# First projection of a hybrid encoder layer: input and weight loads in turn, dummy matmuls ahead, parameters turned behind the loop

## The chip, the core and the metric

The kernel runs on one core of one Trainium2 chip. The metric is device time in microseconds (us) of that core, from the runtime's own clock; a profiled execution has a span (first to last instruction) a little shorter than its time. Engines: TensorE (PE, with its weight loads as PEld), VectorE (DVE), ScalarE (ACT), GpSimd (POOL) and SyncE (SP), which issues most loads.

## The reference

One layer of a streaming encoder runs on two request groups that share the weights: a prompt of 256 positions and 32 sampled positions, 288 columns in all. Everything is float32.

```
xn   = rmsnorm(x, norm_mix_pre)
proj = xn @ w_in      # [u_pool 1024 | z 2048 | xBC 2560 | dt 32]
pool = trailing-mean mixer on u_pool (windows 2, 4, 8, 16), then w_pool
ssd  = Mamba-2 mixer: causal conv + SiLU on xBC = [xs 2048 | B 256 | C 256],
       dt = softplus(.), exact chunked scan, gate silu(z), grouped rmsnorm
x    = x + rmsnorm(concat[pool, ssd] @ w_out, norm_mix_post)
h    = rmsnorm(x, norm_ffn_pre)
x    = x + rmsnorm((silu(gate) * value) @ w_down, norm_ffn_post)
       # [gate | value] = causal conv of width 3 over h @ w_up (2 * 5632 columns)
```

Outputs are the two x and the new histories and states of the convolutions, the pooling and the scan.

## The kernel before

**Tiling.** Features lie on the 128 partitions, the 288 positions in the free dimension. A matrix product is made in three float32r matmuls per 128 x 128 weight block (`mm3`, L162 to L165: high part times high part, high times low, low times high), each with 288 columns. `split_w` (L134) makes the high part of a loaded weight tile on ACT (L146, `whi`) and the low part on DVE (L147, `wlo`); `split_from` (L113) does the same for activations (L120 on ACT, L121 on DVE). The buffers `raw`, `hi` and `lo` of the pool `wpool` come four each; a raw buffer holds 8 KB a partition, 1 MB in all.

**The first projection** gives the columns B (256), C (256) and dt (32) of `w_in`. `project` (L167) runs over five steps of k (2, 2, 4, 4 and 4 blocks of 128 features). In each step it fetches three weight tiles (`fetch_w`, L131, on SP), and before it splits them calls `first_in` for the step behind, which runs `input_tiles` (L292): load of the prompt's columns into `xt` (L294) and of the samples' into `xs_` (L295), both on SP; per 128 features three transposes on TensorE into one PSUM tile, two of 128 rows (L299, L300) and one of the samples' 32 rows (L301); the split with the gain `g_mix_pre`; a copy of the unscaled tile to `xT` (L304), stored to DRAM per step from ACT (L306). The normalization itself is applied later: the sums of squares of each position (`ssum`, L348 and L349 on ACT), root and reciprocal, and three matmuls against the identity (L355) spread them into `rstd`, by which the results are multiplied as they leave PSUM.

The dt columns go through `split_narrow`, which lays high and low part side by side so that two matmuls a k do for three (L185, L186). `parameters` (L309) turns the small parameters, which POOL loads at the start, with ten transposes (L281, L325); it is called ahead of the last step.

**Five PSUM buffers** (`acc_ps`) hold the five results of this projection. They come free as `conv_in` (L377) multiplies them by `rstd`, and only then the next projection, x's columns (`xs_ps`), can begin to accumulate. After that follow, all through `project`: x, z and u columns, the pool mixer, `w_out`, `w_up` and `w_down`.

**Order.** A planner orders the instructions of each engine by priority, readiness and its own estimate of their durations. `tc.keep_in_program_order(ins)` pins an instruction behind the one traced just before it on the same engine. Engines serve their queues in order. At the start POOL clears constants (`ident`, `ones`, `rec`, `scan_one`, `ebuf`), DVE makes `sel`, `pick` and `sel64`, and `warm` lets ACT load its table (L225).

Of the kernel before, what the change touches and what calls it, by code (L numbers as in the profile page):

```python
# [16 lines left out]
P = 128  # L17
TC = {"schedule_with_timeline_sim": True}
D_MODEL = 2048
NP_ = 256  # L20
# [17 lines left out]
EVAC = 100  # L38
SUMS_AFTER = 2
# [6 lines left out]
def body(  # L46
# [81 lines left out]
    def fetch_w(view, kb, nk, c0, nc_):  # L128
        raw = wpool.tile([P, nk, nc_], F32, tag="raw", name="raw")
        with tc.high_priority(offset=ahead[0]):  # L130
            sp.dma_start(out=raw, in_=view[:, kb : kb + nk, c0 : c0 + nc_])  # L131
        return raw

    def split_w(raw, kb, nk, nc_, after=()):  # L134
# [3 lines left out]
        for k in range(0, nk, step):  # L138
# [3 lines left out]
            with ExitStack() as order:  # L142
# [3 lines left out]
                act.activation(hi, raw[:, k : k + n, :], AF.Copy)  # L146
                dve.tensor_tensor(lo, raw[:, k : k + n, :], hi.bitcast(F32), op=ALU.subtract)  # L147
# [3 lines left out]
    def split_narrow(raw, kb, nk, nc_, after):  # L151

        both = xin.tile([P, nk, 2, nc_], F32R, tag="both", bufs=2, name="both")
        with ExitStack() as order:
            order.enter_context(tc.high_priority(offset=ahead[0]))
            for ins in after:
                order.enter_context(tc.issue_after(ins.ins))
            act.activation(both[:, :, 0, :], raw, AF.Copy)
            dve.tensor_tensor(both[:, :, 1, :], raw, both[:, :, 0, :].bitcast(F32), op=ALU.subtract)
        return [(kb + k, both[:, k, :, :].rearrange("p r c -> p (r c)")) for k in range(nk)]  # L160
# [6 lines left out]
    def project(view, groups, acts, ksplit, before=None, done=None, spare=(), hold=(), behind=None):  # L167
# [7 lines left out]
        for i, (kb, n) in enumerate(ksplit):  # L175
# [5 lines left out]
            for raw, (c0, w) in zip(raws, groups):  # L181
                if w < P:
                    for k, both in split_narrow(raw, kb, n, w, after or ()):
                        o = accs[m0][: 2 * w, :]
                        pe.matmul(o, both, acts[k][:, 0, :], start=k == k_first, stop=False)  # L185
                        pe.matmul(o, both, acts[k][:, 1, :], start=False, stop=k == k_last)  # L186
                    continue
# [33 lines left out]
    )  # L221
    eps_t = const.tile([P, 1], F32, name="eps_t")
# [10 lines left out]
    sel = const.tile([HEADS, 2], F32, name="sel")  # L233
    pick = const.tile([HEADS, NX], F32, name="pick")
    id32 = ident[:HEADS, :HEADS]
    dve.tensor_reduce(sel, id32.rearrange("h (t r) -> h r t", r=2), axis=AX.X, op=ALU.add)
    dve.tensor_reduce(pick, id32.rearrange("h (t r) -> h t r", r=2), axis=AX.X, op=ALU.add)
    sel64 = const.tile([HEADS, 2, 64], F32, name="sel64")
    dve.tensor_copy(sel64, sel.unsqueeze(2).broadcast_to([HEADS, 2, 64]))

# [6 lines left out]

    start = ExitStack()
    xin = start.enter_context(tc.tile_pool(name="xin", bufs=1))
# [9 lines left out]
    xs_ = xin.tile([NS, D_MODEL], F32, name="xs_")  # L259
# [24 lines left out]

    g_mix_pre = columns(g0_in, KD, "g0")
# [6 lines left out]
    def input_tiles(kb, n):  # L292
# [3 lines left out]
        for t in range(kb, kb + n):  # L296
            p_ = aux([P, NT], "pt")
            c = slice(t * P, (t + 1) * P)
            pe.transpose(p_[:, 0:P], xt[:, 0, c], ident)  # L299
            pe.transpose(p_[:, P:NP_], xt[:, 1, c], ident)  # L300
            pe.transpose(p_[:, NP_:NT], xs_[:, c], ident[:NS, :NS])  # L301
            a = atile("xn")
            last = split_from(a, p_, g_mix_pre[:, t : t + 1])
            dve.tensor_copy(xT[:, t, :], p_)  # L304
            xn.append(a)
# [844 lines left out]
```

## Time and profile before

| | |
|---|---|
| time, median of 3 runs | 1357.07 us (1357.01 to 1357.39) |
| profiled execution: time | 1357.63 us |
| profiled execution: span | 1355.8 us |
| TensorE busy | 1337.4 us, 99%, 10201 matmuls |
| DVE, ACT, POOL busy | 884.0, 667.0, 237.6 us (65%, 49%, 18%) |
| DMA | 252.13 MB, mean 186 GB/s |
| longest groups | L147 on DVE, 493.8 us (416 times, 1189 ns); L146 on ACT, 427.0 us (416 times, 1028 ns) |

A row of the timeline reads: start, duration, engine, line of the kernel, operation, output from inputs, shape, count. Matmuls are pipelined, so a duration is longer than the distance to the next start; the distance is what a matmul costs. A row of the windows gives, for each engine, busy us and in brackets the number of instructions, then the granted TensorE clock, the share of the DMA engines and GB/s. The chain is the work that ended last, followed back through what released each step.

### The profile page before, as it was taken

The numbers are of one execution on the slowest core, as the hardware profiler recorded it, in microseconds if no ns is written. First come the engines' busy times: TensorE is split into PE (matmuls) and PEld (weight loads), VectorE is DVE, ScalarE is ACT, GpSimd is POOL, SyncE is SP. The second block draws the span as 40 slices with busy tenths as digits, with TensorE's granted clock in tenths as the row PEclk, the third lists the DMA queues.
The fourth block names the chain that finished last, engine by engine and source line by source line (L and its number), as shares of the span: only waits on it lengthen the run. The fifth ranks groups of instructions, "written<-read, shape, count | busy, mean of one in ns | idle before, by whom it ended". The sixth has DMA issues, their size and how long they took to land.

```text
span 1355.8 us, 25731 instructions
## 1 busy us (share of the span) xinstructions
PE 1337.4 (99%) x10201; PEld 1327.3 (98%) x10201; DVE 884.0 (65%) x1515; ACT 667.0 (49%) x997; POOL 237.6 (18%) x394
## 2 busy tenths in 40 slices
PE   8999999999999999999999999999999999999996
PEld 7999999999999999999999999999999999999995
DVE  6898988779644469977666643435666667654443
ACT  6557757446534455644444433334444444454441
POOL 3132112222224310311121100001112112101110
PEclk9999999999999999999999999999999999999998
DMA  8879885565756536866545555555545545576652
GB/s 268 249 190 277 257 245 172 156 220 153 241 180 209 170 111 202 244 180 193 171 158 173 160 155 159 169 179 163 179 156 165 177 156 167 168 226 201 189 163 88
DMA packets 300136, 252.13 MB, mean 186 GB/s; under 512 B 75729, under 2 KB 293051, under 8 KB 299887
## 3 DMA queue, kind: packets, MB, share of 16 engines
q1 hardware_dynamic: 296810, 243.20, 59.2%
q0 software_dynamic: 2320, 4.65, 1.2%
q10 hardware_dynamic: 884, 2.63, 0.5%
q8 instruction: 80, 1.31, 0.4%
q14 instruction: 42, 0.34, 0.1%
HBM read 236.13 MB, written 14.31 MB: 185 GB/s over the span
## 4 chain that ended last, share of the span: by engine, by line
PE 98%; DVE 0%; DMA 0%; SPq 0%; issue 0%; DVEq 0%; ACT 0%
PE acc L163 31%; PE acc L165 31%; PE acc L164 31%; PE pst L852 1%; PE py L562 1%; DMA xt<-in_x_prompt 0%; DVE xr L1108 0%; PE acc_x L164 0%; PE acc_x L165 0%; PE acc_x L163 0%; PE py L564 0%; PE pt L301 0%; PE acc L186 0%; PE pt L299 0%; PE acc L185 0%; PE py L568 0%
## 5 line engine op out<-in xcount | busy, mean ns | idle before, releaser
L147 DVE TENSOR_TENSOR wlo<-raw,whi 128x1024 fp32r<-128x1024 f32 (+1 forms) x416 | 493.8, 1189 | 350.7 <-ACT whi L146 340.2
L146 ACT ACTIVATE whi<-raw 128x1024 fp32r<-128x1024 f32 (+1 forms) x416 | 427.0, 1028 | 505.6 <-PE acc L164 429.5
L163 PE MATMUL acc<-hn,whi 128*128 128x288 f32 x1376 | 404.6, 295 | 0.0
L164 PE MATMUL acc<-hn,whi 128*128 128x288 f32 x1376 | 403.5, 294 | 0.0
L165 PE MATMUL acc<-hn,wlo 128*128 128x288 f32 x1376 | 403.2, 294 | 0.0
L164 PEld LDWEIGHTS acc<-hn,whi 128*128 128x128 f32 x1376 | 259.8, 189 | 0.1
L165 PEld LDWEIGHTS acc<-hn,wlo 128*128 128x128 f32 x1376 | 259.6, 189 | 0.0
L163 PEld LDWEIGHTS acc<-hn,whi 128*128 128x128 f32 x1376 | 257.3, 187 | 0.1
L163 PE MATMUL acc<-xn,whi 128*128 128x288 f32 x704 | 209.5, 299 | 0.0
L163 PE MATMUL acc<-fa,whi 128*128 128x288 f32 x704 | 208.6, 296 | 0.0
L164 PE MATMUL acc<-fa,whi 128*128 128x288 f32 x704 | 208.4, 296 | 0.0
L164 PE MATMUL acc<-xn,whi 128*128 128x288 f32 x704 | 208.2, 297 | 0.0
L165 PE MATMUL acc<-fa,wlo 128*128 128x288 f32 x704 | 208.0, 295 | 0.0
L165 PE MATMUL acc<-xn,wlo 128*128 128x288 f32 x704 | 207.5, 297 | 0.0
L164 PEld LDWEIGHTS acc<-xn,whi 128*128 128x128 f32 x704 | 133.8, 190 | 0.3
L165 PEld LDWEIGHTS acc<-xn,wlo 128*128 128x128 f32 x704 | 133.2, 190 | 0.3
L163 PEld LDWEIGHTS acc<-xn,whi 128*128 128x128 f32 x704 | 132.6, 189 | 0.5
L164 PEld LDWEIGHTS acc<-fa,whi 128*128 128x128 f32 x704 | 132.7, 188 | 0.0
L163 PEld LDWEIGHTS acc<-fa,whi 128*128 128x128 f32 x704 | 132.2, 188 | 0.0
L165 PEld LDWEIGHTS acc<-fa,wlo 128*128 128x128 f32 x704 | 132.0, 188 | 0.0
L944 POOL COPY fc_stage<-ebuf 128x4 f32<-128x4 f32 x88 | 27.9, 317 | 505.7 <-DVE ebuf L943 505.7
L950 DVE SCALAR_TENSOR_TENSOR fc<-ebuf,pf,fc 128x290 f32<-128x290 f32 x176 | 90.3, 517 | 2.8 <-ACT fc L948 0.2
(310 smaller groups left out, 1621.6 us busy)
## 6 DMA issues: line engine op xcount, KB each, us to landing
raw<-in_w_up SPq DMA_DIRECT2D x80, 1024.0 KB, 5.2
raw<-in_w_in SPq DMA_DIRECT2D x40, 1024.0 KB, 6.1
raw<-in_w_down SPq DMA_DIRECT2D x32, 1024.0 KB, 5.4
raw<-in_w_out SPq DMA_DIRECT2D x24, 1024.0 KB, 5.9
raw<-in_w_down SPq DMA_DIRECT2D x16, 768.0 KB, 4.6
raw<-in_w_up SPq DMA_DIRECT2D x14, 512.0 KB, 4.2
gb<-g_d SPq DMA_DIRECT2D x8, 832.0 KB, 5.0
raw<-in_w_in SPq DMA_DIRECT2D x6, 512.0 KB, 6.5
```

The lines of the kernel that those rows point to most:

```text
L146: act.activation(hi, raw[:, k : k + n, :], AF.Copy)
L147: dve.tensor_tensor(lo, raw[:, k : k + n, :], hi.bitcast(F32), op=ALU.subtract)
L163: pe.matmul(out, wh, a[:, 0, :], start=start, stop=False)
L164: pe.matmul(out, wh, a[:, 1, :], start=False, stop=False)
L165: pe.matmul(out, wl, a[:, 0, :], start=False, stop=stop)
L562: ins = pe.matmul(y[c, 0:256], xw[:, 0, f_], m[:, h, 0:256], start=True, stop=False)
L852: ins = pe.matmul(st[:, o, :], x_, btok[:, gi, b, :], start=b != 1, stop=b != 0)
L944: pool.tensor_copy(fc_stage[:, :, :, i], e[:, 256:324].rearrange("p (s c) -> p s c", c=34)[:, :, 0:2])
L950: dve.scalar_tensor_tensor(c, e[:, r_ : r_ + 290], pf[:, r_, i : i + 1], c, op0=ALU.mult, op1=ALU.add)
```

## The change

- The first projection is written out as a loop of its own, over ten steps of k (`FIRST`: 1, 1, 1, 1, then six of 2). B and C are loaded as one tile of 512 columns. All loads are issued at the start on SP, pinned in turn: x, weights, x, weights, and so on; the rest of the samples behind the second, and all dt columns in one load behind the sixth weight load.
- The four raw buffers hold all of B and C. The dt split is made once, in the eighth step, and its matmuls follow the gathered k, then those of each step.
- The samples lie at partitions 96 to 127 of `xs_`, and zeros above them (the first two tiles' columns cleared by DVE, the others by POOL); their transpose becomes a matmul against the last 32 columns of the identity. Their first two tiles are loaded from ACT's queue.
- Twelve dummy matmuls on `busy`, a copy of `ones` made by DVE, are put on TensorE: seven ahead of the gain's transpose, five behind the first tile's.
- Tiles are turned one step ahead. In the first k the products of the high part come first, then tile 1 is turned, then the products of the low part. The first four steps are pinned on TensorE (in part), ACT and DVE.
- `xT` is stored in three pieces instead of five. `parameters` is called behind the loop, `sel`, `pick` and `sel64` are made behind it, and the three matmuls of `rstd` use all 128 rows.

```diff
+FIRST = ((0, 1), (1, 1), (2, 1), (3, 1), (4, 2), (6, 2), (8, 2), (10, 2), (12, 2), (14, 2))
+STORES = {3: 0, 9: 4, 15: 10}
+BUSY = (7, 5)
...
+    busy = xin.tile([P, NT], F32R, name="busy")
+    for o, n in BLK:
+        tc.keep_in_program_order(dve.tensor_copy(busy[:, o : o + n], ones[:, 0:n]))
+
+    xs_ = xin.tile([P, D_MODEL], F32, name="xs_")
+    tc.keep_in_program_order(dve.memset(xs_[: P - NS, : 2 * P], 0.0))
...
-    tc.keep_in_program_order(act.activation(warm, eps_t, AF.Copy))
...
+    pool.memset(xs_[: P - NS, 2 * P :], 0.0)
...
+    tc.keep_in_program_order(act.dma_start(out=xs_[P - NS :, : 2 * P], in_=x_sample[0][:, : 2 * P]))
+    tc.keep_in_program_order(act.activation(warm, eps_t, AF.Copy))
+    busy_ps = aux([P, NT], "busy_ps")
+
+    def keep_busy(n):
+
+        for _ in range(n):
+            tc.keep_in_program_order(pe.matmul(busy_ps, busy[:, 0:P], busy, start=True, stop=True))
...
+    keep_busy(BUSY[0])
     g_mix_pre = columns(g0_in, KD, "g0")
...
+    def input_load(kb, n):
         c = slice(kb * P, (kb + n) * P)
-        sp.dma_start(out=xt[:, :, c], in_=xpv[:, :, c])
-        sp.dma_start(out=xs_[:, c], in_=x_sample[0][:, c])
...
+        tc.keep_in_program_order(sp.dma_start(out=xt[:, :, c], in_=xpv[:, :, c]))
+
+    def input_tile(t):
+        p_ = aux([P, NT], "pt")
+        c = slice(t * P, (t + 1) * P)
+        pin = tc.keep_in_program_order if t < 4 else lambda ins: ins
+        pin(pe.transpose(p_[:, 0:P], xt[:, 0, c], ident))
+        pin(pe.transpose(p_[:, P:NP_], xt[:, 1, c], ident))
+        pin(pe.matmul(p_[:, NP_:NT], xs_[:, c], ident[:, P - NS :], start=True, stop=True))
+        a = atile("xn")
+        xn.append(a)
+
+        def split():
+            pin(act.activation(a[:, 0, :], p_, AF.Copy, scale=g_mix_pre[:, t : t + 1]))
+            pin(dve.scalar_tensor_tensor(
+                a[:, 1, :], p_, g_mix_pre[:, t : t + 1], a[:, 0, :].bitcast(F32), op0=ALU.mult, op1=ALU.subtract
+            ))
+
+        def keep():
+            pin(dve.tensor_copy(xT[:, t, :], p_))
+            if t in STORES:
+                c = slice(STORES[t], t + 1)
+                act.dma_start(out=xT_d[:, c, :], in_=xT[:, c, :])
+
+        return split, keep
...
+    first = [acc_ps.tile([P, NT], F32, tag="acc", name="acc") for _ in range(5)]
+    raws = [wpool.tile([P, 4, NB], F32, tag="raw", name="raw") for _ in range(4)]
+    raw_dt = xin.tile([P, KD, HEADS], F32, name="raw_dt")
+    for i, (kb, n) in enumerate(FIRST):
+        input_load(kb, n)
+        k = slice(kb, kb + n)
+        tc.keep_in_program_order(
+            sp.dma_start(out=raws[kb // 4][:, kb % 4 : kb % 4 + n, :], in_=win[:, k, O_B : O_B + NB])
+        )
+        if i == 1:
+            c = slice(2 * P, D_MODEL)
+            tc.keep_in_program_order(sp.dma_start(out=xs_[P - NS :, c], in_=x_sample[0][:, c]))
+        if i == 5:
+            tc.keep_in_program_order(sp.dma_start(out=raw_dt, in_=win[:, :, O_B + NB : O_B + NB + HEADS]))
+
+    def first_tiles(i):
+        return [input_tile(t) for t in range(FIRST[i][0], sum(FIRST[i]))] if i < len(FIRST) else []
+
+    prm = []
+    dt_parts = []
+    steps = first_tiles(0)
+    keep_busy(BUSY[1])
+    for i, (kb, n) in enumerate(FIRST):
+        pin = i < 4
+        ahead_steps = first_tiles(i + 1) if i else []
+        for split, _ in steps:
+            split()
+        parts = split_w(raws[kb // 4][:, kb % 4 : kb % 4 + n, :], kb, n, NB, pin=pin)
+        for _, keep in steps:
+            keep()
+        narrow = split_narrow(raw_dt, 0, KD, HEADS, False) if i + 3 == len(FIRST) else ()
+        dt_parts.extend(narrow)
+        if not i:
+            (_, hi, lo), = parts.pop()
+            for w, r in ((hi, 0), (hi, 1), (lo, 0)):
+                if w is lo:
+                    ahead_steps = first_tiles(1)
+                for m in range(4):
+                    tc.keep_in_program_order(pe.matmul(
+                        first[m], w[:, m * P : (m + 1) * P], xn[0][:, r, :], start=w is hi and not r, stop=False
+                    ))
+        for part in parts:
+            for m in range(4):
+                c = slice(m * P, (m + 1) * P)
+                for k, hi, lo in part:
+                    mm3(first[m], hi[:, c], lo[:, c], xn[k], k == 0, k == KD - 1)
+        while dt_parts and dt_parts[0][0] < kb + n:
+            k, both = dt_parts.pop(0)
+            o = first[4][: 2 * HEADS, :]
+            pe.matmul(o, both, xn[k][:, 0, :], start=k == 0, stop=False)
+            pe.matmul(o, both, xn[k][:, 1, :], start=False, stop=k == KD - 1)
+        steps = ahead_steps
+    prm.extend(parameters())
...
+    tc.keep_in_program_order(dve.tensor_reduce(sel, id32.rearrange("h (t r) -> h r t", r=2), axis=AX.X, op=ALU.add))
+    tc.keep_in_program_order(dve.tensor_reduce(pick, id32.rearrange("h (t r) -> h t r", r=2), axis=AX.X, op=ALU.add))
...
-            p_[:, o : o + n], rs[:n, b : b + 1].broadcast_to([n, P]), ident[:n, :n], start=True, stop=True
+        pe.matmul(p_[:, o : o + n], rs[:, b : b + 1].broadcast_to([P, P]), ident[:, P - n :], start=True, stop=True)
```

More of the change, by code (lines that the diff above doesn't have):

```diff
@@ L181, in project @@
             for raw, (c0, w) in zip(raws, groups):
[L182 to L187, printed above, removed]
                 parts = split_w(raw, kb, n, w, ((after or ()) if m0 else ()) + (hold if i else ()))
@@ L290, in body @@
     xT_d = dram.tile([P, KD, NT], F32, name="xT_d")
-    def input_tiles(kb, n):
+    def input_load(kb, n):
         c = slice(kb * P, (kb + n) * P)
-        sp.dma_start(out=xt[:, :, c], in_=xpv[:, :, c])
-        sp.dma_start(out=xs_[:, c], in_=x_sample[0][:, c])
[L296 to L305, printed above, removed]
-        act.dma_start(out=xT_d[:, kb : kb + n, :], in_=xT[:, kb : kb + n, :])
-        return last
+        tc.keep_in_program_order(sp.dma_start(out=xt[:, :, c], in_=xpv[:, :, c]))
[19 more added lines that the diff above has]
+        return split, keep
     def parameters():
```

62 lines of the change are left out of this document (27 added, 35 removed).

## The prediction

> **What bounds the kernel now.** First the page: how busy TensorE is over the span, and the chain that ended last.
>
> ```profile
> PE 1337.4 (99%) x10201; PEld 1327.3 (98%) x10201; DVE 884.0 (65%) x1515; ACT 667.0 (49%) x997; POOL 237.6 (18%) x394
> ...
> PE 98%; DVE 0%; DMA 0%; SPq 0%; issue 0%; DVEq 0%; ACT 0%
> ```
>
> TensorE is the chain. What is gained at the start moves everything behind it, as long as the stream stays fed. Then the windows of 10 us each, whose first bracket counts matmuls:
>
> ```profile
> 0.00:10.00 10.00, 4.73 (x20) 3.81 (x21) 5.77 (x12) 4.47 (x9) 8.54 (x45) 1.00 0.73 215
> 10.00:20.00 10.00, 10.00 (x61) 9.28 (x60) 6.26 (x14) 3.79 (x8) 3.38 (x7) 1.00 1.07 329
> 20.00:30.00 10.00, 10.00 (x70) 8.99 (x69) 6.45 (x13) 8.35 (x13) 0.00 (x0) 1.00 0.91 259
> 50.00:60.00 10.00, 10.00 (x77) 10.00 (x77) 8.57 (x18) 6.60 (x10) 2.85 (x5) 1.00 1.10 329
> ```
>
> The settled rate is 77 in 10 us; the first 30 us fall short of it. Busy time hides this, counts show it. Why, the chain in order of time shows (start, length):
>
> ```profile
> 6.99 0.45 PE pt L299
> ...
> 9.38 0.54 PE acc L165
> ...
> 13.23 0.24 PE acc L163
> 13.47 0.24 PE acc L164
> 13.71 0.29 PE acc L165 x2
> 14.00 0.13 PE acc L163
> ```
>
> Until 13.7 us a matmul takes 0.24 us, then 0.13: half clock. (The column of granted clock reads 1.00 there; I go by the spacing.) And from the timeline of TensorE, one input tile, then the nearest row to its new form, six matmuls of 128, 128 and 32 columns over 128 rows:
>
> ```profile
> 21.62 0.27 PE L299 MATMUL pt<-ident,xt 128*128 128x128 f32 x1
> 21.73 0.27 PE L300 MATMUL pt<-ident,xt 128*128 128x128 f32 x1
> 21.93 0.24 PE L301 MATMUL pt<-ident,xs__137 32*128 32x32 f32 x1
> 22.11 0.40 PE L165 MATMUL acc<-xn,wlo 128*128 128x288 f32 x1
> 22.35 0.29 PE L163 MATMUL acc<-xn,whi 128*128 128x288 f32 x1
> ...
> 494.13 0.39 PE L852 MATMUL pst<-btok,xw 128*128 128x128 f32 x2
> 494.36 0.81 PE L601 MATMUL rm<-ident,rm 128*128 128x128 f32 x6
> 495.00 0.47 PE L852 MATMUL pst<-btok,xw 128*128 128x128 f32 x2
> ```
>
> **The stage in terms.** The last matmul of the first projection starts near 52.5 us. From there to 60 us some 56 matmuls of 0.133 us follow; 273 hi/lo matmuls start before 60, 192 are the stage's own, so 25 or 26 of the next projection came early. Less those 3.4 us, the stage ends at 49.2. Its work: 192 + 32 matmuls x 0.133 = 29.8; 16 tiles; parameter transposes 0.9 (rows L281, L325); the three L355 matmuls 0.9. A tile costs 22.11 - 21.62 = 0.49 plus 0.11 by which the matmul behind it is late (0.24 against 0.13): 0.60, in all 9.6. Sum 41.2; the other 8.0 us are the start: nothing to multiply before 7.3 us, half clock until 13.7.
>
> **Sample rows at partitions 96 to 127, zeros above.** L301 over 32 rows becomes a matmul over 128 rows with 32 columns. In the row at 494.36 six take 0.64; a pair of 128 columns takes 0.23 (494.13 to 494.36), so the pair of 32 columns 0.18. A tile becomes 0.11 + 0.11 + 0.18 = 0.40, 0.2 less: 3.0 us over the fifteen tiles that lie behind the first matmul. Bounds: 0.14 a tile less (a late matmul behind it, as now, though no partial-row load causes it) to 0.26 (0.03 for the first of the pair): 2.1 to 3.9 us. The rs matmuls get the same form: 0.9 to 0.6.
>
> **First data.** The weight split waits for its load now: issued 1.82, ACT's L146 starts at 6.12. Bytes ahead and with it: 0.55 MB, which the windows' rates reach at 4.5 us; landing lags by 1.6. After, one x tile (0.13 MB), B and C for one k (0.26), g and a piece of samples (0.04) come first: 0.43 MB and instruction fetch 0.05, at 4.0 us, landed 5.4. The x tile needs 2.8 + 1.2 = 4.0. Tile 0 is turned by 4.9 at half clock, ACT's xn 0.5 (L120) to 5.45, hi split 0.63 to 6.1: first matmul 6.15 instead of 7.3.
>
> **Dummy matmuls.** Seven run from 1.8 (ones is written at 1.16; three copies) to 3.5, five between tile 0 and the first product; both lie in time in which TensorE waits for data, so they cost nothing. If the copies are late they cost all of it, 12 x 0.24 = 2.9 us (rival 1). When the clock rises: in this trace 4.3 us after matmuls became continuous (9.38 to 13.71), 6.7 us after TensorE did (6.99). Counted from 1.8, that is 6.1 to 8.5; counted from 6.15, 10.5. At half clock half the time is lost, so from 6.15 to 8.5 costs 1.2, to 10.5 costs 2.2.
>
> [...]
>
> **Loads.** SP issues 22 loads one behind the other, about 0.45 us each, done near 11 us; the four raw buffers hold all the weights, so none waits for a buffer, where now L131 is issued at 7.5 and 9.2, just as a split (L147) frees one. Bytes in order at 0.33 MB/us (windows of 10 to 25 us) with 1.4 us lag: k = 1 lands at 6.8, 2 at 8.7, 3 at 10.0, 4 and 5 at 12.7, 6 and 7 at 15.7, 8 and 9 at 21.5 (behind dt and the xT_d store), 14 and 15 near 30.6. A chunk of two needs xn 1.0, hi 1.06, lo 1.22: 3.3 us; TensorE spends 24 x 0.133 + 0.8 = 4.0 on one. Only k = 4 and 5 come tight: tiles turned 13.4, lo at 16.5, needed 15.7: 0.8 lost, 0.4 if the clock is late.
>
> **Moved work.** Parameters' transposes stay 0.9. Their loads now lie on POOL behind a memset of 1792 columns (0.31 for 326, so 1.7 us): landed by 22.3 instead of 20.6, needed past 40. The 2.1 us of sel's copy leave DVE's start. ACT issues one load more before its table load (1.28 us): to 3.0, needed at 4.9. DVE's pinned reductions stand behind the parameters' copies; behind them waits rstd's reciprocal, 0.3 us, covered by the last chunk. dt: 24 matmuls gather behind k = 11, sum unchanged.
>
> **The sum.** From 6.15: 29.8 + 15 x 0.40 + 0.9 + 0.6 = 37.3, so 43.5; cold clock 1.2 to 2.2, tight chunk 0.8 to 0.4: 45.4 to 46.1. Against 49.2: 3.1 to 3.8 us, nearer the upper end if the first seven dummies count: 3.8. The profiled execution took 1357.63 (span 1355.8 and 1.8 around it), 0.56 over the median 1357.07: 1353.8 there, **1353.3** as a median.
>
> **Rival 1, the copies starve (1 in 5).** The dummies' source is a copy on DVE while POOL clears tiles. The timeline has just that:
>
> ```profile
> 1.80 2.09 DVE L239 COPY sel<-sel 32x128 f32<-32x128 f32 x1
> ...
> 2.53 1.29 POOL L245 MEMSET ebuf<- 128x326 f32 x4
> 3.77 0.69 POOL L254 DMA_DIRECT2D pb_in<-in_state_ssd_conv  x1
> ```
>
> A copy of 128 columns ended only as POOL's memsets did. With the 1.7 us memset added that is 5.6: dummies 5.9 to 7.6, tile 0 to 8.7, first matmul 9.9, and 9.9 + 37.3 = 47.2 with up to 1.9 cold: 47.3 to 49.1, a gain of 0.1 to 1.9, say 1356. Against it: ones is ready at 1.16, and POOL pauses at 1.24 before its next select, so the copies can come first. [...]
>
> **Rival 2, the clock rises no sooner (1 in 8).** If transposes between bursts keep it low until 13.7: 3.8 cold instead of 1.2 to 2.2, partly within the tight chunk: 47.0, gain 2.2, 1354.9.
>
> **Rival 3, slower (1 in 8).** The planner puts the sums of squares (L348, L349: 1.91 + 0.19 three times) among the splits, now at 25 to 33 us:
>
> ```profile
> 25.04 1.91 ACT L348 ACTIVATE junk<-xt 128x2048 f32<-128x2048 f32 x1
> ```
>
> They need all of x, which then lands with the last loads, near 30.6; now, by the same count of bytes, near 18. ACT serves in order: if a square is queued ahead of the split of k = 10 and 11, these come at 30.6 + 2.1 + 3.3 = 36 and are due at 28.8: 7.2 late, net 3.4 slower, 1360.5. Ahead of k = 8 and 9 it is 7 slower. Queued ahead of k = 12 (due 36, behind the gathered dt matmuls) it costs nothing; from k = 10 and earlier on it decides. For it: the place in the present order. Against: the planner places a square only once it counts x as landed.
>
> **How the numbers follow.** The forecast has 0.50, rivals 0.20, 0.12 and 0.12, a gain over 5 us (tiles at their lower bound, clock at 6.1) 0.06. No change means within 0.2%, 2.7 us, about what a measurement of this kernel can tell. Faster: forecast and the large gain, with rival 2's better third, 0.58. Same: rival 1, the rest of rival 2 and of the forecast's lower edge, 0.30. Slower 0.12. The range runs from a gain of 5.6 (1351.5) through rivals 2 and 1 to 1357.6; outside are rival 3 and the best few.
>
> **What would show it.** Right: dummies before 2 us; first acc matmul near 6; spacing 0.13 before 10.5; tile to next matmul 0.40; first acc product of the next projection 3 to 4 us earlier; counts per 10 us near 77 from 20 on. Wrong: a long copy of busy on DVE, ACT standing before a square for DMA xt, or a gap past 60 us where the stream now has none.

## The result, and the profile after

The change made the kernel slower: 1367.64 us median of six runs (1366.23 to 1373.04) against 1357.04 in the same session, ratio 1.0088 with a 95% interval of 1.0078 to 1.0098. The forecast was 1353.3, in a range of 1351.5 to 1357.6. The profiled execution took 1366.23 us (span 1364.2), 8.6 more than that of before, and is the one read here. It is the fastest of the six: the median has 2.0 us more of loss against before's, which no trace shows.

The page first: TensorE's busy share and its share of the chain.

```profile
PE 1340.9 (98%) x10229; PEld 1332.4 (98%) x10229; DVE 882.1 (65%) x1515; ACT 665.8 (49%) x993; POOL 232.2 (17%) x395
...
PE 92%; DVE 3%; DMA 2%; SPq 1%; issue 1%; ACT 1%; POOL 0%; DVEq 0%; ACTq 0%; POOLq 0%
```

The chain no longer runs through TensorE alone: VectorE, a transfer and SyncE's issues have come into it. The windows say where (matmuls in the first bracket, granted clock third from the end):

```profile
0.00:10.00 10.00, 8.20 (x33) 7.43 (x34) 2.64 (x9) 3.12 (x6) 9.14 (x44) 1.00 0.79 217
10.00:20.00 10.00, 8.31 (x64) 7.84 (x63) 7.61 (x13) 4.84 (x8) 4.32 (x8) 1.00 1.06 282
20.00:30.00 10.00, 7.41 (x43) 7.39 (x44) 6.28 (x12) 5.35 (x9) 0.00 (x0) 0.66 1.06 363
50.00:60.00 10.00, 7.07 (x57) 6.76 (x56) 7.66 (x25) 4.09 (x7) 2.99 (x9) 1.00 0.69 197
```

Two holes: 43 matmuls between 20 and 30 us, at a granted clock of 0.66, and 57 between 50 and 60, where before had 70 and 77. To place the loss exactly I number the matmuls that accumulate into `acc` buffers, from 0 on, and compare the start of each with that of the same number in before. The 40th starts 2.3 us sooner than before, the 80th 3.6 later, the 215th 1.7 later, the 224th (the first of the next projection) 6.5 later, the 1200th 8.7 later; from there to the end the difference stays at 8.6. So three places: **a stall near 20 us, the loop's end, and something between the 500th and the 1200th.**

**The start itself is as forecast.** From the timeline:

```profile
1.20 0.54 DVE L227 CAST busy<-ones 128x128 fp32r<-128x128 f32 x3 [1.20 <-POOL rec L236]
...
6.41 2.24 PE L391 MATMUL acc<-xn,whi 128*128 128x288 f32 x8
...
12.15 0.27 PE L307 MATMUL pt<-ident,xt 128*128 128x128 f32 x1
...
12.51 0.77 PE L170 MATMUL acc<-xn,whi 128*128 128x288 f32 x4
```

The copies of `busy` are done by 1.74, the first product starts at 6.41 (forecast 6.15), and a tile costs 12.51 - 12.15 = 0.36 (forecast 0.40).

**First hole.** ScalarE's timeline; a bracket gives the idle time ahead and what ended it:

```profile
16.41 0.48 ACT L314 ACTIVATE xn<-pt,g 128x288 fp32r<-128x288 f32 x1
21.63 0.36 ACTq L323 DMA_DIRECT2D xT_d<-xT  x1
22.04 0.50 ACT L314 ACTIVATE xn<-pt,g 128x288 fp32r<-128x288 f32 x1 [5.14 <-DMA raw<-in_w_in]
```

ScalarE stands from 16.9 to 21.6 at the issue of the first store of `xT_d`. The store copies tiles 0 to 3, and VectorE had made the last of these copies by 14.8:

```profile
14.38 0.45 DVE L320 COPY xT<-pt 128x288 f32<-128x288 f32 x1
```

The store goes only at 21.63, just after the load of weights k = 8, 9 has landed (21.55). In the trace the loads of SyncE and the stores of ScalarE take eight semaphores in turn (100, 101, 103, 105, 106, 116, 117, 118), and this store has 101, which this load used last; ScalarE's wait for it is over at 21.58. It waits for a transfer that it has nothing to do with. In every run below that leaves the store on ScalarE's queue, it goes 0.07 to 0.08 us behind the landing of the transfer that had its semaphore before. In the same way SyncE's load of weights at 8.49 has 117, the semaphore of the sample load, which landed at 8.48. So at most eight of the loads that are issued at the start are under way at a time in this trace. TensorE waits for the split behind the store (`xn`, 4.1 us from start to start) and comes back at half clock, 0.24 us a matmul until 27.0. Rows k = 6, 7 had landed by 15.4; it is not their weights that it waits for.

That the load landed so late has its cause in SyncE's queue:

```profile
8.91 0.95 SPq L366 DMA_DIRECT2D raw_dt<-in_w_in  x1
9.90 4.93 SPq L301 DMA_DIRECT2D xt<-in_x_prompt  x1
14.88 0.47 SPq L360 DMA_DIRECT2D raw<-in_w_in  x1
```

The dt load is 2048 rows of 128 bytes. Its own issue takes 0.95 us; the next one takes 4.93.

**Second hole**, the loop's end:

```profile
52.18 0.79 PE L426 MATMUL prs<-ident,rs 128*128 128x128 f32 x6
...
53.07 0.76 DVE L344 COPY pf<-ptf 128x264 f32<-128x264 f32 x2
...
53.94 0.43 DVE L428 COPY rstd<-prs 128x288 f32<-128x288 f32 x1
...
55.75 0.37 PE L170 MATMUL acc<-xn,whi 128*128 128x288 f32 x1 [2.78 <-DVE ebuf L450]
```

The matmuls that spread `rstd` stand behind the parameters' ten transposes, and the copy of `rstd` behind their copies, a split (1.24 us) and the pinned reductions. All five accumulators wait for `rstd`, so TensorE starts nothing for 3.1 us. In before, `rstd` was copied amid the loop:

```profile
43.45 0.46 DVE L359 COPY rstd<-prs 128x288 f32<-128x288 f32 x1
```

### The profile page after: what moved, and what is told of

Read it like the earlier page. It is cut to its first block, busy times and chain, and to the rows that moved or that the text cites. A ratio compares the mean times of both kernels' runs of the same rounds, so it can differ in the third digit from the quotient of the medians.

```text
span 1364.2 us, 25768 instructions
## 1 busy us (share of the span) xinstructions
PE 1340.9 (98%) x10229; PEld 1332.4 (98%) x10229; DVE 882.1 (65%) x1515; ACT 665.8 (49%) x993; POOL 232.2 (17%) x395
## 4 chain that ended last, share of the span: by engine, by line
PE 92%; DVE 3%; DMA 2%; SPq 1%; issue 1%; ACT 1%; POOL 0%; DVEq 0%; ACTq 0%; POOLq 0%
PE acc L170 29%; PE acc L172 29%; PE acc L171 29%; PE pst L921 1%; DMA xs_d<-blocks 1%; DVE wlo L153 1%; PE py L631 1%; DVE conv L462 1%; DMA raw<-in_w_in 0%; SPq L301 0%; DMA xs__91<-in_x_sample 0%; SPq L210 0%; SPq L583 0%; DMA h<-in_state_ssd 0%; DVE xr L1177 0%
## 5 line engine op out<-in xcount | busy, mean ns | idle before, releaser
L170 PE MATMUL acc<-xn,whi 128*128 128x288 f32 x700 | 205.2, 299 | 7.2 <-ACT xn L314 3.8
L171 PE MATMUL acc<-xn,whi 128*128 128x288 f32 x700 | 205.4, 296 | 0.5 <-DVE xn L315 0.5
L172 PE MATMUL acc<-xn,wlo 128*128 128x288 f32 x700 | 204.5, 296 | 0.0
L170 PEld LDWEIGHTS acc<-xn,whi 128*128 128x128 f32 x700 | 130.3, 188 | 8.2 <-ACT xn L314 4.0
L171 PEld LDWEIGHTS acc<-xn,whi 128*128 128x128 f32 x700 | 132.5, 190 | 0.8 <-DVE xn L315 0.7
L1008 POOL COPY ebuf<-pf 128x2 f32<-128x2 f32 x88 | 74.0, 840 | 113.7 <-DVE fc L1019 54.1
```

The costliest lines, as they stand in the source:

```text
L170: pe.matmul(out, wh, a[:, 0, :], start=start, stop=False)
L171: pe.matmul(out, wh, a[:, 1, :], start=False, stop=False)
L172: pe.matmul(out, wl, a[:, 0, :], start=False, stop=stop)
L1008: pool.tensor_copy(e[:, 258:260], pf[:, 4:6, i])
```

## The experiments

All times are medians in us, with before at 1356.8 to 1357.2 in the same session. "Lag" is the start of the nth accumulating matmul in the profiled execution less that of the kernel before; minus is sooner. "Profiled" is the time of that one execution: where it is far from the median, the lags are those of an unusually fast or slow execution.

| kernel | lag 80th | 215th | 300th | 1500th | profiled | time |
|---|---|---|---|---|---|---|
| the change | +3.6 | +1.7 | +6.5 | +8.6 | 1366.2 | 1367.6 |
| store on GpSimd | -3.2 | +0.5 | +6.3 | +6.5 | 1364.1 | 1364.0 |
| parameters in the loop | +3.4 | +3.1 | +3.2 | +5.2 | 1362.5 | 1364.6 |
| both | -3.3 | +2.8 | +2.8 | +6.8 | 1364.2 | 1364.0 |
| dt load last | -1.4 | -3.2 | +3.3 | +8.2 | 1365.6 | 1365.7 |
| rstd ahead of the last step | +2.5 | +1.2 | +2.1 | +1.7 | 1359.1 | 1360.1 |
| dt last, rstd ahead | -1.8 | -2.2 | -1.4 | +7.0 | 1364.3 | 1364.3 |
| dt last, parameters in the loop | -2.5 | -1.8 | -1.8 | +3.9 | 1361.4 | 1361.0 |
| dt last, wide load in its place | +0.4 | -1.0 | +5.0 | +8.2 | 1365.8 | 1368.6 |
| rstd ahead, dt in quarters | +3.7 | +2.5 | +3.3 | +3.0 | 1360.6 | 1360.2 |
| the same, two block buffers | +4.0 | +2.8 | +3.6 | +3.7 | 1361.3 | 1361.7 |
| dt last, rstd ahead, two block buffers | -1.7 | -2.8 | -2.0 | +4.2 | 1361.9 | 1358.6 |
| before, two block buffers | -0.8 | -0.8 | -0.8 | +4.9 | 1362.6 | 1362.6 |
| dt last, rstd ahead, lead 400 | +0.8 | -0.4 | +0.4 | +9.3 | 1366.6 | 1363.0 |
| dt last, rstd ahead, lead 100 | -1.5 | -2.5 | -1.7 | +0.7 | 1358.1 | 1358.2 |
| dt last, rstd ahead, store on GpSimd | -2.8 | -2.5 | -1.7 | +5.5 | 1363.0 | 1363.8 |
| dt last, rstd ahead, parameters in the loop | -0.3 | -0.5 | -0.5 | +2.7 | 1360.1 | 1362.3 |
| dt last, rstd ahead, two block buffers, lead 100 | -1.6 | -2.8 | -2.0 | -2.2 | 1355.4 | 1356.8 |
| before, lead 100 | -0.4 | -0.4 | -0.4 | +0.2 | 1357.8 | 1356.9 |

The two versions of before begin as before does, and yet run 0.8 and 0.4 us ahead: their clock rose at 12.3 and 12.9 us, that of before at 13.6. So a lag under 1 us can come from the execution and says nothing of the edit.

### The store or the loads

```diff
-                act.dma_start(out=xT_d[:, c, :], in_=xT[:, c, :])
+                pool.dma_start(out=xT_d[:, c, :], in_=xT[:, c, :])
```

> Edit: the three stores of xT_d are issued by GpSimd's queue instead of ScalarE's; all else as in the changed kernel. In the changed kernel ScalarE stands from 16.8 to 21.6 us behind the first of these stores, whose queue waits for the landing of the load of weights k=8,9, and TensorE then stands 4.1 us for xn. Theory S (it is the store's place on ScalarE's queue that costs the time): ScalarE goes on at 16.8, the stall at 18.5 to 22.6 is gone but for 0.5 to 1.5 us, the 80th accumulating matmul starts some 4 to 6 us sooner than the changed kernel's (about 30 instead of 34), total 1361 to 1364. The late rstd at 52 us stays. Theory L (rival: the loads themselves are late, for the small-row dt load holds SyncE's issue for 4.9 us; the store only stands in front of a wait that would come anyway): the stall ends no more than 1.5 us sooner, since raw of k=8,9 lands at 21.5 and the weights of 6,7 near 16; total 1366 to 1368.

Measured 1364.0. Both theories hold, one after the other. The store goes at 15.57, the stall at it is gone and the 80th matmul starts 6.8 us sooner; by the 120th 5.5 of them are lost again. The chain of that run, in order of time (start, length):

```profile
15.41 10.20 DMA raw<-in_w_in
25.69 1.06 ACT whi L152
26.74 0.40 ACT xn L314
27.19 0.54 PE acc L170 x2
```

Now the weights of k = 10, 11 are late, for SyncE's issue behind the dt load still took from 8.89 to 14.34. The store's wait covered late loads.

```diff
-        if i == 5:
+        if i == 9:
             tc.keep_in_program_order(sp.dma_start(out=raw_dt, ...
...
-        narrow = split_narrow(...) if i + 3 == len(FIRST) else ()
+        narrow = split_narrow(...) if i + 1 == len(FIRST) else ()
```

> Edit: the dt columns are loaded behind the last load of B and C weights instead of one load behind six chunks, and split in the loop's last step; the store of xT_d stays on ScalarE's queue and the parameters behind the loop. Theory L (the 2048 rows of 128 bytes of the dt load hold up SyncE's queue for 4.9 us and every load behind it): the loads of k=8,9 and later are issued some 5 us sooner and land 3 to 6 us sooner, ScalarE's wait at the store ends by 17 to 18 us, and the total falls by 3 to 6 us, to 1361.5 to 1364.5. Theory S' (the store waits for its slot behind whatever load was issued eight transfers before it, and the transfers are limited by the bytes that the memory hands out, not by the issue): the landing of k=8,9 moves by less than 2 us, the stall too, and the total stays within 2 us of 1367.6; the dt matmuls then come last and add up to 1 us.

SyncE's queue in that run:

```profile
8.53 0.37 SPq L360 DMA_DIRECT2D raw<-in_w_in  x1
8.94 0.47 SPq L301 DMA_DIRECT2D xt<-in_x_prompt  x1
9.49 0.43 SPq L360 DMA_DIRECT2D raw<-in_w_in  x1
...
16.12 0.91 SPq L366 DMA_DIRECT2D raw_dt<-in_w_in  x1
17.93 11.24 SPq L134 DMA_DIRECT2D raw<-in_w_in  x3
```

The load of k = 8, 9 is issued at 9.49 instead of 14.88 and lands at 17.85 instead of 21.55. The store, still on ScalarE, goes at 18.60, and still not when its data is ready (13.9): it now follows a load of x, which had its semaphore before and landed at 18.52.

```profile
16.43 0.48 ACT L314 ACTIVATE xn<-pt,g 128x288 fp32r<-128x288 f32 x1
18.60 0.36 ACTq L323 DMA_DIRECT2D xT_d<-xT  x1
```

ScalarE stands 1.7 us there instead of 4.7. At the 215th matmul the kernel is 3.2 us ahead of before, as much as was forecast for the stage. The total (1365.7) hardly shows it, and misses what was expected: 4.9 us go at the loop's end, where `rstd` is now even later against a loop that ends sooner, 1.6 right behind it, mostly at half clock, and another 4.9 behind the 550th matmul.

### Rows or bytes

```diff
+    wide = xin.tile([P, 1, NB], F32, name="wide")
...
+        if i == 5:
+            tc.keep_in_program_order(sp.dma_start(out=wide, in_=win[:, 0:1, 0:NB]))
         if i == 9:
```

> Edit: the dt columns loaded last, as in the run before on that, and in their old place a load of the same 262 kB in 128 rows of 2048 bytes, whose data nobody uses. Theory N (it is the number of rows, 2048 of 128 bytes, that holds the queue): SyncE's next issue behind it takes about 0.5 us instead of 4.9, the loads of k=8,9 and later land 1 to 2 us later than without it, the 180th matmul is 1.5 to 3 us ahead of the kernel before, total within 1.5 us of the run with the dt load last (1364 to 1367). Theory B (bytes: any load of 262 kB in that place pushes the weights back by as much as the dt load does): the next issue takes 3 us or more, the 80th matmul is 2 to 4 us behind the kernel before, total 1366 to 1368.

```profile
8.58 0.51 SPq L367 DMA_DIRECT2D wide<-in_w_in  x1
9.14 0.44 SPq L301 DMA_DIRECT2D xt<-in_x_prompt  x1
9.62 0.47 SPq L361 DMA_DIRECT2D raw<-in_w_in  x1
```

The issue behind 262 kB in 128 rows takes 0.44 us, and k = 8, 9 land at 18.02, 0.2 later than without it. So it is the rows. (The total was missed: 1368.6, through the late `rstd`, which is still there, and the later loss. So was the lead at the 180th matmul, 0.8 us: a gap of 1.9 us and 3.4 us of half clock lie ahead of it.) In the packet records of the changed kernel's first 60 us a row of 128 bytes takes one DMA engine 14.8 ns in the mean and a row of 2048 bytes 100 ns: 8.6 against 20.5 bytes a ns. By that, as an estimate, the 2048 rows occupy all sixteen engines for 1.9 us, and from 15 to 20 us the changed kernel moves 243 GB/s where the run with the dt load last moves 333. Why rows hold up the issue behind them, no run shows.

Then the same rows in four loads of 512 (with rstd's block ahead, see below):

```diff
-        if i == 5:
-            tc.keep_in_program_order(sp.dma_start(out=raw_dt, ...
+        if 4 <= i < 8:
+            k = slice(4 * (i - 4), 4 * (i - 3))
+            tc.keep_in_program_order(sp.dma_start(out=raw_dt[:, k, :], in_=win[:, k, ...
```

> Edit: as the run with rstd's block ahead of the last step, and the dt columns loaded in four loads of 512 rows, one behind each of the loads of four chunks from k=4,5 on (the kernel before loaded them in five loads of 256 to 512 rows). Theory N (it is one load of 2048 rows that holds the queue; the bytes and the rows as such do little): no issue behind a quarter takes over 1.5 us, the 180th and the 300th matmul start 1.5 to 3 us sooner than in the kernel before, against 0.7 and 2.1 us later with the one load; total 1354 to 1356.5, or 2 to 6 us more if a loss between the 550th and the 1500th matmul comes with this version's order. Rival (all rows have to be fetched in between anyway, so quarters only spread the same hold): the 180th matmul stays within 1 us of the run with one load.

My theory that one long load was at fault fell; quarters spread the same hold, as the rival had it. No single issue took over 1.5 us, but the last weight load was issued at 19.1 (19.3 in the changed kernel, 15.4 with the dt load last), and the total stayed at 1360.2 (1360.1 with one load). The lag of the 180th matmul rose from 0.7 to 1.9, a little more than the rival allowed; 0.6 us of that is the clock, at half for 4.5 us behind the gap here and for 3.4 with one load. ScalarE stood at the same store again, for another load this time:

```profile
21.62 0.36 ACTq L323 DMA_DIRECT2D xT_d<-xT  x1
22.03 0.50 ACT L314 ACTIVATE xn<-pt,g 128x288 fp32r<-128x288 f32 x1 [4.77 <-DMA xt<-in_x_prompt]
```

What costs here is rows of 128 bytes ahead of weights that are due, in one piece or four. One dt load instead of four bought nothing (1360.1 against 1360.2); the rows are 128 bytes long either way.

### rstd at the loop's end

```diff
+        pin = i < 4; i == len(FIRST) - 2 and prm.extend(parameters())
...
-    prm.extend(parameters())
```

> Edit: the parameters' transposes and copies are called within the loop of the first projection again, ahead of its last-but-one step, instead of behind the loop; all else as in the changed kernel. By the planned order the two matmuls that spread rstd then stand ahead of the last chunk's matmuls, as in the kernel before. Theory R (the step of 4.7 us between the 215th and the 224th accumulating matmul is rstd, which comes 53.9 us behind the parameters' copies on VectorE, with all accumulators of TensorE waiting for it): that gap falls under 1.5 us and the total falls by 3 to 5 us, to 1362.5 to 1364.5; the stall at 18.5 to 22.6 stays. Rival P (TensorE would have waited there anyway, for the evacuation of its five accumulators or for the next weights, so that an early rstd only moves the wait): the gap falls by less than 2 us and the total stays within 1.5 us of 1367.6.

1364.6: the gap is gone (lag 3.1 at the 215th, 3.1 at the 224th), but 2 us go to the parameters inside the loop, between the 180th and 200th, as they did in before. With the store on GpSimd as well:

> Edit: both of the foregoing, stores of xT_d on GpSimd's queue and the parameters called within the loop. If the two causes are separate and stand one behind the other on the path, the gains add up: 1367.6 less 4 to 6 less 3 to 5, so 1357 to 1360.5, and what is left above 1357.0 less the 2 us gained up to the 40th matmul is the 2 us that the trace loses between the 500th and the 1200th matmul. If the loads are what binds (theory L), a gain of the first part is lost again before the loop's end, and the sum is that of the second edit alone, 1362 to 1364. If both causes and the later loss hang on the same things, it is faster than the kernel before: 1352 to 1356.

1364.0. The gain of the store was lost again before the loop's end, as theory L said. Both edits together cure symptoms.

Then the block of `ssum`, `rs`, `prs` and `rstd` written ahead of the last step, with the parameters left behind the loop:

```diff
+        if i == len(FIRST) - 1:
+            rstd = spread_rstd()
```

> Edit: the sums of squares, the reciprocal root and the two matmuls that spread rstd are written ahead of the loop's last step; the parameters stay behind the loop, the dt load one load behind six chunks. Theory R (TensorE waits 3.1 us at the loop's end for rstd alone, not for the parameters): the gap between the 215th and the 224th accumulating matmul falls from 5.9 to about 1.3 us, as in the kernel before and in the run with the parameters in the loop, and without the 2 us that the parameters' transposes took inside the loop there; the 300th matmul is then 1.5 to 2.5 us behind the kernel before, total 1361.5 to 1363.5. Rival (the projection behind needs the parameters, so the wait comes back one stage later): the 300th matmul gains 4 us, but by the 1500th 3 of them are lost again, total 1366 to 1367.5.

1360.1, ratio 1.0023 (1.0014 to 1.0033): of the 10.6 us that the change lost, 7.6 come back from this one move, more than was expected. Only part of that is the wait at the loop's end: in the profiled executions 4.4 us come back by the 300th matmul, and 2.5 more because the loss behind it (2.1 us in the change) is not there, which nobody had forecast. The `prs` matmuls run at 46.2, `rstd` is copied at 46.97, the four `ebuf` are written from 48.5, and the 224th matmul follows without a gap. The rival, that the parameters are needed at once, is refuted: from the 300th matmul to the 1500th the lag falls from 2.1 to 1.7.

> Edit: the dt columns loaded last and split in the last step, and rstd's block ahead of the last step; parameters behind the loop. Theory L+R (the forecast's gain of 3 us is there once the load of small rows no longer holds the queue, and rstd no longer comes last): the 215th and the 300th matmul both start 2 to 3.5 us sooner than in the kernel before, total 1353.5 to 1355. Rival (the late parameters and the other order of the loads behind the loop cost time of their own between the 500th and the 1200th matmul, as in the changed kernel, 2 to 5 us): the 300th matmul is 2 to 3.5 us ahead, the end is not, total 1356 to 1360.

> Edit: the dt columns loaded last and split in the last step, and the parameters called within the loop. Theory L+R: at the 300th matmul some 0.5 to 1.5 us ahead of the kernel before, since the parameters' transposes cost 1.2 to 2 us inside the loop. If late parameters make the later loss, none follows here, total 1355.5 to 1357; if the later loss belongs to the order of loads and copies that the planner makes anew for each version, 2 to 5 us follow at some place between the 500th and the 1500th matmul, total 1358 to 1361.

They took 1364.3 and 1361.0. Both are 1.4 to 1.8 us ahead of before at the 300th matmul, where the change is 6.5 behind: late weights and late `rstd` are most of what stood between the forecast and the trace up to there. Not all: 2 to 3.5 us were expected there of the first, 3 to 4 at the 224th by the forecast, and what holds the rest back was not tested. And both are slower than before at the end; 1364.3 is more than either theory gave.

### The later loss

These runs vary the work behind the first projection and keep its start nearly the same. First two buffers for the transposed blocks, which VectorE writes and SyncE stores:

```diff
-        s = pool_.tile([P, NT], F32, tag="blocks", bufs=1, name="blocks")
+        s = pool_.tile([P, NT], F32, tag="blocks", bufs=n, name="blocks")
```

with n = 2 for `b_d` and `xs_d`.

> Edit: as the run with the dt load last and rstd's block ahead of the last step (1.4 us ahead of the kernel before at the 300th matmul, 7.0 us behind it at the 1500th), and two buffers for the transposed blocks. Theory O: the 8.4 us lost between the 900th and the 1500th matmul shrink to under 3, total 1355 to 1358.5. Rival: they shrink by under 2 us, or the loss moves to another place of the same size; total 1362 to 1365.

> Edit: as the run with the dt load in quarters, and two buffers instead of one for the transposed blocks that are stored to b_d and xs_d behind the first projection. Theory O (where time is lost between the 550th and the 1500th matmul, VectorE stands at the transpose into the one buffer until its last store has landed, and the split of the next weights stands behind it): no TensorE wait for wlo over 0.8 us behind the 300th matmul, the lead of the 300th matmul is there at the end too, total 1354 to 1356.5. Rival (the later loss is another wait: the weights' own landing, or the reload of xs_d): the loss stays within 1 us of the same version with one buffer.

> Edit: the kernel before, with two buffers for the transposed blocks and nothing else. TensorE waits for nothing behind its first projection in the kernel before, so by theory O nothing is to be had from it: within 1.5 us of 1357.0, either way. If it comes out 3 us or more slower, a new order of the engines' queues costs that much by itself, without any change at the start: the kernel before then stands in a good order by chance or by trial, and part of what the change loses behind the 500th matmul is that.

The control shows what an order can be worth: **the kernel before, given only a spare buffer, loses 5.6 us** (1362.6, ratio 1.0037, 1.0025 to 1.0049), at two places near 130 and 194 us, where before's TensorE waits for nothing. Its waits behind the first projection:

```profile
PE acc L165 <- DVE wlo L147: 2.5, 1, 2.5
PE py L562 <- DVE m L550: 1.1, 1, 1.1
```

The version with quarters, which lost nothing there, has nothing from the buffer either (1361.7 against 1360.2). In the run with dt last and two buffers, 2.0 us of lead hold to the 1200th matmul, and then one place costs 6.5. (This execution, 1361.9, is the slowest of ten; the fastest took 1356.3, the median is 1358.6, just over theory O's range, and the loss in the trace, 6.2 us, is that of neither theory.) The chain there:

```profile
185.15 0.38 SPq L608
185.58 5.93 DMA xk<-xs_d
192.04 0.43 issue
192.47 0.52 DVE conv L466
192.99 1.15 DVE wlo L153
194.18 0.61 PE acc L172
```

VectorE's product with the reload `xk` of the stored blocks, in this run and then in before:

```profile
191.60 0.96 DVE L612 TENSOR_TENSOR xw<-xk,tok 128x768 f32<-128x768 f32 x1 [3.01 <-DMA xk<-xs_d]
```

```profile
188.76 0.96 DVE L539 TENSOR_TENSOR xw<-xk,tok 128x768 f32<-128x768 f32 x1 [0.21 <-DMA xk<-xs_d]
```

VectorE comes to this product at 188.6 in both. A load of weights (1 MB) stands ahead of the reload in SyncE's queue in both, but it is issued at 183.65 here and at 181.38 in before, and the reload lands at 191.5 here and at 188.7 there. VectorE waits 3.0 us, the split `wlo` of the next weights stands behind it in order, TensorE stands 4.0 us for the split and runs at half clock until 199. The planner works out the whole order anew for each version, and such places open and close. But the ten executions of this one order lie 5.5 us apart, while 22 of before in the same session lie 2.5 apart: with one order, too, such a place seems to open in some executions and not in others. With one trace per kernel that is not shown.

To tell order from an early start, the lead that the planner gives to later weights (`ahead[0]`, 200) was changed, with the start of the run "dt last, rstd ahead":

> Edit: as the run with the dt load last and rstd's block ahead of the last step (1364.3 us; 1.4 us ahead of the kernel before at the 300th matmul, 7.0 behind at the 1500th), and the loads and splits of later weights are given a lead of 400 instead of 200 in the planner's order. Theory O (the loss behind the 550th matmul belongs to the place where the planner puts the splits of weights among VectorE's other work, and the loads of weights among SyncE's others): the 300th matmul stays 1 to 2.5 us ahead, the loss behind it changes by 3 us or more, down most likely, since the splits stand sooner: total 1354 to 1361. Rival E (an earlier start as such runs into the later loads, whatever the order): the loss stays at 8.4 us within 2, total 1362 to 1366.

> Edit: the same version with a lead of 100 instead of 200. Theory O: the 300th matmul 1 to 2.5 us ahead, the loss behind it different by 3 us or more from 8.4; splits that stand later should lose more, total 1364 to 1372, though a later load of weights leaves SyncE's queue free for the reload of xs_d. Rival E: the loss stays at 8.4 us within 2, total 1362 to 1366.

> Edit: the same version with the lead of 200, and the stores of xT_d on GpSimd's queue; VectorE's order is the same instruction by instruction as with ScalarE's. Theory O: the same order gives the same later loss, 8.4 us within 2, total 1362 to 1366. Theory S (the store still holds ScalarE up at the start): the 60th to 120th matmul start some 1 to 2 us sooner than with the store on ScalarE's queue (19.99 and 31.36 us); if they do not, the store costs nothing once the dt load is out of the way.

> Edit: the same version with the lead of 200, the store on ScalarE's queue, and the parameters called within the loop. Theory O: about 0.5 to 1 us less lead at the 300th matmul, a different order behind it, and so a loss that differs from 8.4 us by 3 us or more, total 1354 to 1361. Rival E: loss of 8.4 us within 2, total 1363 to 1367.

From the 300th to the 1500th matmul the profiled executions lose 8.9 (lead 400), 8.4 (200) and 2.4 (100); with the parameters in the loop 3.2; and 7.1 with the store on GpSimd, where VectorE's order is the same as in the 8.4. The medians bear out the lead of 100 (1358.2 against 1364.3, though its ten executions run from 1355.4 to 1361.1); the parameters in the loop are 2.0 faster by median, and the lead of 400 (1363.0) cannot be told from 200 and came out as rival E had it. So a change of order alone takes away 6 us of loss with the same early start, and in the control it makes 5.6 without one. That each of the losses is the order's, and none the early start's, is not shown. The sign against the lead was the opposite of what I expected. The store on GpSimd made the 80th matmul 1.0 us sooner but the 215th only 0.3: with the dt load out of the way the store costs next to nothing.

> Edit: the dt load last, rstd's block ahead of the last step, parameters behind the loop, two buffers for the transposed blocks, and a lead of 100 instead of 200 for later weights. With two buffers and a lead of 200 the 2.0 us of lead held to the 1200th matmul and were lost at one place near 190 us, where a load of weights stood ahead of the reload of xs_d in SyncE's queue and VectorE waited 3 us for that; with the lead of 100 and one buffer that place cost 0.6 us. Theory O: both together keep the lead, the 1500th matmul 1 to 2.2 us ahead of the kernel before, total 1354.5 to 1356.3, as good as what was forecast for the change. Rival: another place of 2 us or more opens up somewhere, total 1357 to 1362.

> Edit: the kernel before, with a lead of 100 instead of 200 for later weights and nothing else; VectorE's order differs in few places. If the lead of 100 were a gain of its own, this comes out 2 us or more under 1357.0; by theory O it has nothing to win there, since TensorE waits for nothing behind the first projection: 1356.5 to 1358.5, or slower where the other order opens a gap.

1356.78 for the first (1355.43 to 1357.77, 11 runs), against 1356.85: ratio 0.9996 (0.9987 to 1.0005). TensorE's waits, from 5 to 330 us:

```profile
PE acc L170 <- ACT xn L314: 0.8, 1, 0.8
PE acc L171 <- DVE xn L315: 0.3, 1, 0.3
```

Theory O holds in the profiled execution: a lead of 2.2 us to the end, and 1355.43 us. But that is the fastest of the eleven. The median is 1.3 above it and outside theory O's range, so the best version is level with before, not better. The control with lead 100 stays at 1356.9.

## Why the prediction was wrong, step by step

- **Dummies, copies (rival 1), tile cost, first product: right.** 1.80, no long copy, 0.36, 6.41. The row of 2.09 us that spoke for the rival did not decide: the three copies took 0.54 together, from 1.20 on, and GpSimd's long memsets began at 2.58.
- **Clock (rival 2): right.** The spacing falls to 0.13 at 10.0, near the upper of my two times, so 1.8 us of half-clock cost. That it fits so well has some luck in it: in the sixteen other runs that begin with these dummies the clock record has the rise anywhere from 5.5 to 10.6 us. What I did not count was that it can be lost again: 4.1 us from one matmul to the next, and it is at half from 20.1 to 27.0.
- **"SP issues 22 loads one behind the other, about 0.45 us each, done near 11 us ... none waits for a buffer": wrong.** The last was issued at 19.3. This is the step that failed first. I looked at buffers and missed two other things that a queue waits for, the semaphore's former transfer and the hold by small rows (4.93 us in one issue). I had costed dt by its bytes.
- **The landing list: right, by luck where it matters** (k = 6, 7 forecast 15.7, split at 15.45; 8, 9 forecast 21.5, landed 21.55). The 21.5 counted the bytes of dt and of the first `xT_d` store ahead of 8, 9. The store came behind them; and with the dt load last 8, 9 landed at 17.85, with its bytes in long rows at 18.02. So bytes make it some 18, and the hold of the queue, which the list did not have, the other 3.5 us. What followed from the list was wrong too. "Only k = 4 and 5 come tight": by my own figures 8, 9 were due at 15.7 + 2 x 4.0 = 23.7 and ready at 21.5 + 3.3 = 24.8. I stopped after the first tight chunk. That would have been 1.1 us.
- **The stores of `xT_d` were counted as bytes only.** Five became three and the first moved behind k = 3, into ScalarE's queue ahead of the splits. Who waits behind it was not asked: ScalarE stood 4.7 us there. This and the loads cost 5.9 us between the 40th and the 80th matmul. Rival 3 named the mechanism, ScalarE held in order by a late load, but with the wrong instruction: no wait of TensorE goes back to the squares.
- **"Needed past 40", "covered by the last chunk": wrong.** The reciprocal was indeed ready at 41. But its spreading matmuls stand behind the call that was moved, and the next user of everything is `rstd`. I costed what `parameters` issues and not what was traced behind it. 4.7 us.
- **"Or a gap past 60 us where the stream now has none"** was named as a sign of being wrong and given no price. It was 2.1 us net in the change, 0 to 9 in its variants. The control shows that a spare buffer alone can cost 5.6: the kernel before lies in an order without gaps, and another order can give that up. A rival for it belonged in the sum. Which place of the changed kernel's order makes its 2.1 us stays open.

The gain of 3 us that was summed for the start exists up to the 215th matmul: 3.2 us with the dt load last. With `rstd` ahead too, 1.9 to 2.6 us are left in five of seven versions at the first product of the next projection, where the forecast had 3 to 4. It is smaller than each of the two waits that came with the change.

## What to carry to other kernels

When an issue is moved into another queue position, ask for every DMA in that queue what it waits for besides its data, and which compute instruction stands behind it. Count a load's rows as well as its bytes, and put loads of short rows behind those that are due. When a change moves a call behind a loop, look at what is written after that call and now comes later with it: here the one value that all accumulators wait for. And where a planner orders the whole program, run the kernel before with harmless edits first: how far the time moves (5.6 us here with one, nothing with the other) is the price that a new order can have.

## What the runs showed of the hardware

- Transfers from SyncE and ScalarE share eight semaphores in turn; through one of them a store whose data was ready at 14.8 us waited until 21.6 for an unrelated load, and ScalarE stood 4.7 us at it.
- 2048 rows of 128 bytes held the next issue on their queue for 4.93 us; the same bytes in 128 rows, 0.44 us.
- A gap in TensorE's stream can be paid twice: in the changed kernel with 4.1 us from one matmul to the next, and with half clock from 20.13 to 26.96. By its clock record the rise at 9.89 us, this fall and the next rise lie 3 and 2 steps of 3.41 us apart; in before's the rise at 13.64 and the fall at 1344.84, behind the last matmul, lie 390 apart. The stretches at half clock amid the stream are 3.4 us long (in the run with the wide load) or 6.8 (in the changed kernel), and begin at the end of such a step, not of the gap: in the run with the wide load a gap from 17.9 to 19.8 us was enough (half clock from 19.9), in before with two block buffers the clock fell at 196.6, when the gap of 192.7 to 195.5 was over, and a gap of 2.1 us in the run with dt last and rstd ahead cost nothing.
